# Exp over three PSUM banks instead of two, with single banks for VectorE's scores and for the outputs

## The chip, the cores and the metric

The kernel runs on one core of a Trainium2 chip. Its engines work side by side, each through its own instructions in a fixed order: TensorE (PE in the profile) multiplies matrices and writes to PSUM, ScalarE (ACT) computes functions such as exp, VectorE (DVE) and GpSimd (POOL) compute element by element, and SyncE (SP) here only issues transfers. PSUM, where the products land, has eight banks; one holds 512 fp32 values in each of 128 partitions. Engines wait for each other through semaphores.

The metric is the device time in microseconds (us), the median of several executions. The kernel before takes 386.97 us (386.77 to 387.01 in three runs). The profile is of one more execution, and its span of 384.9 us is what its tables and times refer to.

## What is computed

Attention with grouped heads: batch 8, 8 query heads, 2 key and value heads, 1024 positions, 64 values per head.

```python
scale = 1.0 / np.sqrt(head_dim)                      # head_dim = 64
for g in range(n_kv_heads):                          # 2 groups of 4 query heads
    # q_group: (8, 4, 1024, 64); k_group, v_group: (8, 1, 1024, 64)
    scores = scale * np.matmul(q_group, k_group.transpose(0, 1, 3, 2))
    scores_max = np.max(scores, axis=-1, keepdims=True)
    attn = np.exp(scores - scores_max)
    attn = attn / (np.sum(attn, axis=-1, keepdims=True) + 1e-08)
    output[:, q_start:q_end, :, :] = np.matmul(attn, v_group)
```

The kernel leaves out the subtraction of the maximum, which cancels in the quotient and isn't needed for scores of this size.

## The kernel before

The work is cut into 128 *jobs*: a batch, a query head and one half of its queries (512). A job has eight *cells*, one for each 128 keys. For a cell, TensorE makes 128 x 512 scores (one bank of PSUM), one of two engines takes their exp, and TensorE multiplies the result with the values, in four matmuls of 65 columns (64 values and a column of ones, which gives the sum). When all eight cells of a job are added up, VectorE divides by the sum.

The exp is the larger part of the work, and is shared between two engines:

- *A cells* go to ScalarE, two at a time: a tile of two PSUM banks, one ACTIVATE of 1024 columns.
- *D cells* go to VectorE. A first step (P below) turns the score into the bits of a bf16 number near the exp, by one multiply-add with an integer result. Then a correction, a *chain* of steps on a group of ten cells at a time: z is the low seven bits ("and"), y a linear function of z ("line", on GpSimd), y becomes z times y ("prod"), and y is added to the bits ("add").

The order of all this is made beforehand in Python, by a loop that keeps a time for each engine and always takes what can start first. The constants at the top say how many cells a tile of ScalarE has, and how many banks there are for VectorE's scores and for outputs:

```python
A_CELLS, D_BANKS, O_BANKS = (2, 2), 2, 2      # 2 + 2 + 2 + 2 = 8 banks
GROUP, PARTS = 10, 2
CHAIN = ("and", "line", "prod", "add")
ON_POOL = ("line",)

def part(step, m):          # "prod0": the first half of the group's cells
    n = step[-1]
    return slice(0, m) if not n.isdigit() else slice(m * int(n) // PARTS, m * (int(n) + 1) // PARTS)
# ... make_plan: times used for the order
    QK, PV, P1, NORM = 0.216, 0.1225, 0.603, 0.555
    EXP = (0.05, 0.4268)
    FOUR, TWO, POOL_ONE = (0.20, 0.133), (0.16, 0.27), (0.25, 0.43)
    COST = {"and": FOUR, "line": POOL_ONE, "prod": TWO, "add": TWO}
    LIVE_A, LIVE_D, PENDING, PER_JOB, LEAD, RAMP, AHEAD, FIRST_PV = 28, 5, 16, 2, 6, 6, 0.04, 2.0
# ...
```

What the engines run, in the order that was made:

```python
    def score(cell, kind, n, slot, col):                     # TensorE
        # ... kind "A": column col of a tile of ScalarE, else a bank of VectorE
        nc.tensor.matmul(dst, lhsT=ksets[b % 2][:, h // HPG, side, c * 128 : (c + 1) * 128],
                         rhs=qT[(b, h)], start=True, stop=True)

    def exps(n, cells):                                      # ScalarE
        act = nc.scalar.activation(out=pt[:, 0:m], in_=psum.pop(("A", n))[:, 0:m],
                                   func=AF.Exp, scale=scale)

    def exp_bits(cell, n, g, slot):                          # VectorE, P
        nc.vector.tensor_scalar(out=groups[g][:, slot], in0=psum.pop(cell),
            scalar1=bits_scale, scalar2=bits_bias, op0=ALU.mult, op1=ALU.add)

    def exp_curve(g, m, step):                               # the chain
        eng = nc.gpsimd if step in ON_POOL else nc.vector
        # ... and:  z  = pd & 0x7F              (tensor_scalar)
        # ... line: y  = z * CURVE_A / 128 + CURVE_B   (tensor_scalar)
        # ... prod: y  = z * y                  (tensor_tensor)
        # ... add:  pd = pd + y                 (tensor_tensor)

    def output_mms(s, cell, opens, closes, bk):              # TensorE
        for qs in range(NQS):                                # 4
            nc.tensor.matmul(ops_of[s][:, qs, :], lhsT=p_of[cell][:, qs * 128 : (qs + 1) * 128],
                             rhs=vsets[b % 2][:, h // HPG, c, :], ...)

    def normalise(s):                                        # VectorE, RN
        nc.vector.reciprocal(out=rec, in_=o[:, :, D])
        nc.vector.tensor_tensor(out=stage[(b, h)][:, :, side, :], in0=o[:, :, 0:D],
                                in1=rec.unsqueeze(2).to_broadcast([128, NQS, D]), op=ALU.mult)
```

Queries and keys come from HBM as bf16 copies and are turned by transposing transfers; keys are then placed by `place_k` (on SyncE's queue) in sets that have zeros in the other half of the rows. The results of ScalarE lie in a ring in SBUF (`p_ring`), from which TensorE reads them. The first head is loaded in another way, through transposes on TensorE that use PSUM banks which are free at that time (`first_loads`).

Of the kernel before, what the change touches and what calls it, by code (L numbers as in the profile page):

```python
# [11 lines left out]

CURVE_A, CURVE_B = 0.32988085, -0.33401025

A_CELLS, D_BANKS, O_BANKS = (2, 2), 2, 2
GROUP, PARTS = 10, 2
CHAIN = ("and", "line", "prod", "add")
ON_POOL = ("line",)

def part(step, m):  # L20

# [4 lines left out]
def make_plan(nj, nkc):  # L26
# [6 lines left out]

    QK, PV, P1, NORM = 0.216, 0.1225, 0.603, 0.555
    EXP = (0.05, 0.4268)
    FOUR, TWO, POOL_ONE = (0.20, 0.133), (0.16, 0.27), (0.25, 0.43)
    COST = {"and": FOUR, "line": POOL_ONE, "prod": TWO, "add": TWO}
    FROM_PE, FROM_PV, FROM_ACT, FROM_DVE, FROM_POOL = 0.21, 0.16, 0.165, 0.10, 0.15
    LIVE_A, LIVE_D, PENDING, PER_JOB, LEAD, RAMP, AHEAD, FIRST_PV = 28, 5, 16, 2, 6, 6, 0.04, 2.0
    INF = 1e9  # L40
    FIRST_TURN, FIRST_LOAD, EACH_LOAD = 3.3, 4.5, 4.2
    ops = []
    pe = act = dve = 0.0
# [22 lines left out]
    while normed < nj:  # L66
        best = None
# [2 lines left out]
        lead = min(LEAD, job_a // RAMP)  # L70
        job_d = max(job_d, job_a + lead)
        while job_d < nj and (
            taken[job_d] >= PER_JOB or not todo[job_d]
        ):
            job_d += 1
        if job_a < nj:
# [7 lines left out]
        if job_d < nj and job_d <= job_a + lead + 1 and pending < PENDING:  # L84
            if cur or live["D"] < LIVE_D:
                t = max(pe, min(bank), loaded(job_d))
                if t < INF:
                    best = min(best or (INF,), (t, 2, "qk", 1, t))
# [10 lines left out]
        for q, p, kind in ((normq, 0, "norm"), (p1q, 1, "p1"), (chainq, 2, "chain")):  # L99
            if q:  # L100
                at = q[0][0]
                if kind != "chain" or CHAIN[q[0][3]] not in ON_POOL:
                    at = max(dve, at)
                best = min(best or (INF,), (at, p, kind, 0))
        if cur and job_d >= nj and not p1q:
            best = min(best or (INF,), (dve, 9, "flush", 0))
        t, _, kind, arg = best[:4]
# [32 lines left out]
        elif kind == "open":  # L140
            o = first_free(obank_free)
            obank[arg] = o
            obank_free[o] = INF
            open_jobs.append(arg)
            rem[arg] = list(range(nkc))
            next_job += 1
        elif kind == "pv":
            s, c = arg
            cell = s * nkc + c
            opens = len(rem[s]) == nkc  # L150
            rem[s].remove(c)
            done = not rem[s]
            ops.append((t, "pv", s, cell, opens, done, obank[s]))
            pe = t + PV
            h = home[cell]
            uses[h] -= 1
            if not uses[h]:
                live[h[0]] -= 1
            if done:
                open_jobs.remove(s)  # L160
                normq.append((pe + FROM_PV, s))
        elif kind == "norm":
            s = normq.pop(0)[1]
            ops.append((t, "norm", s))
            dve = t + NORM
            obank_free[obank[s]] = dve + FROM_DVE
            normed += 1
        elif kind == "p1":
            _, cell, k = p1q.pop(0)
            if not cur:  # L170
                d_id += 1
                live["D"] += 1
            ops.append((t, "p1", cell, k, d_id, len(cur)))
            dve = t + P1
            bank[k] = dve + FROM_DVE
            cur.append(cell)
            home[cell] = ("D", d_id)
            if len(cur) == GROUP:
                chainq.append((dve, d_id, cur, 0))
                cur = []  # L180
        elif kind == "flush":
            chainq.append((dve, d_id, cur, 0))
            cur = []
        else:
            _, g, cells, step = chainq.pop(0)
# [4 lines left out]
            dve = end if name not in ON_POOL else dve  # L190
            if step + 1 < len(CHAIN):
                at = end
                if (name in ON_POOL) != (CHAIN[step + 1] in ON_POOL):
                    at += FROM_POOL if name in ON_POOL else FROM_DVE
                chainq.insert(0, (at, g, cells, step + 1))
# [9 lines left out]
def kernel(  # L205
# [27 lines left out]
    PIECE = 512  # L233
    WARM = 30
    CAST_GAP = 3.0
    P_TILES = 28
    POOL_DMA = 1.0
    OBSERVE = 8
    scale = 1.0 / math.sqrt(D)
    bits_scale = 128.0 * scale * math.log2(math.e)  # L240
    bits_bias = 128.0 * 127.0
# [17 lines left out]
    first_pool = ctx.enter_context(tc.tile_pool(name="firstp", bufs=1))  # L259
    qT_pool = ctx.enter_context(tc.tile_pool(name="qTpool", bufs=10))  # L260
    kT_pool = ctx.enter_context(tc.tile_pool(name="kTpool", bufs=4))
    pd_pool = ctx.enter_context(tc.tile_pool(name="pdpool", bufs=5))
    tmp_pool = ctx.enter_context(tc.tile_pool(name="tmppool", bufs=2))
    ostage_pool = ctx.enter_context(tc.tile_pool(name="ostage", bufs=6))
    recip_pool = ctx.enter_context(tc.tile_pool(name="recip", bufs=10))
# [29 lines left out]
    def at(t, f, *args):  # L295
        events.append((t, len(events), f, args))
# [59 lines left out]
    def first_loads():  # L356
# [86 lines left out]
    def score(cell, kind, n, slot, col):  # L443
        b, h, side = jobs[cell // NKC]
        c = cell % NKC
        if kind == "A":
            if col == 0:
                psum[("A", n)] = apools[slot].tile([128, 2, QBS], FP32, name=f"aps{slot}")
# [3 lines left out]
        last_score[0] = nc.tensor.matmul(  # L452
            dst,
            lhsT=ksets[b % 2][:, h // HPG, side, c * 128 : (c + 1) * 128],
            rhs=qT[(b, h)],
            start=True,
            stop=True,
        ).ins

    def exps(n, cells):  # L460
        pt = p_ring[:, n % P_TILES]
        m = len(cells)
        act = nc.scalar.activation(  # L463
            out=pt[:, 0:m], in_=psum.pop(("A", n))[:, 0:m], func=AF.Exp, scale=scale
        )

        exp_ins.append(act.ins)
        if n >= P_TILES and n % OBSERVE == 0:
# [18 lines left out]
    def exp_curve(g, m, step):  # L487
# [7 lines left out]
        if step.startswith("and"):  # L495
            eng.tensor_scalar(  # L496
                out=z, in0=pd, scalar1=0x7F, scalar2=None, op0=ALU.bitwise_and
            )
# [71 lines left out]
    for b in range(B):  # L570
        for h in range(H):
# [8 lines left out]
            if h % HPG == 0:  # L580
# [4 lines left out]
                    at(th - 11.0 - 15.0 * spare + n, transpose_k, b, g, n)  # L585
                for side in range(2):
                    for parity in range(2):
                        at(th - 6.0 - 9.0 * spare, place_k, b, g, side, parity)
# [46 lines left out]
```

## Time and profile before

| what | value |
|---|---|
| device time, median of 3 | 386.97 us |
| span of the profile | 384.9 us |
| A cells, in ACTIVATEs | 812 in 406 |
| D cells, in groups | 212 in 22 |
| normalisations | 128 |
| granted TensorE clock | full speed |

The page of the profile gives, for each engine, its busy time; the share of the span by engine in the chain of work that ended last, which is followed back from the last instruction; and, for each group of instructions, the line, the engine, what it writes and reads, the count, the busy time and mean duration of one, and the idle time of the engine just before them with what ended it. Instructions of one engine can overlap, so the busy time of a group can be less than the count times the mean. The names: `aps` are ScalarE's score tiles, `dps` VectorE's score banks, `ops` the output banks, `pd` the groups of bits, `ost` the normalised output.

### The profile page before, as it was taken

To read this page: it belongs to the slowest core of one execution; us is meant where nothing else is said; L and a number is where in the kernel's file an instruction comes from. 1 tells how busy PE (TensorE), PEld (TensorE's weight loads), DVE (VectorE), ACT (ScalarE), POOL (GpSimd) and SP (SyncE) were. 2 spreads that over 40 slices of the span, in tenths; PEclk is the share of its full clock that TensorE was granted. 3 is DMA by queue.
4 is the path that set the end of the run, shared out by engine and by line. 5 is a ranking of instruction groups with operands and counts; after the bars stand their busy time and mean duration, and the time that the engine had idled before them with its cause. 6 is when DMAs were issued, how large, how long until landed. Compare 5 with 4: busy or idle time off the path is not lost.

```text
span 384.9 us, 12057 instructions
## 1 busy us (share of the span) xinstructions
PE 368.1 (96%) x5172; PEld 234.5 (61%) x5172; DVE 350.1 (91%) x544; ACT 375.1 (97%) x411; POOL 165.3 (43%) x147
## 2 busy tenths in 40 slices
PE   8879999999999999999999999999999999999985
PEld 6425565656666666666666565666566566666654
DVE  4879999999999999999999999999999999999692
ACT  5999999999999999999999999999999999999994
POOL 5394571716246171625535252535445261531410
PEclk9999999999999999999999999999999999999998
DMA  8888979597859769595865949486584756621213
GB/s 137 152 130 141 141 138 173 113 129 148 128 111 134 132 109 141 123 138 85 151 123 126 125 90 169 74 150 113 119 143 109 111 100 113 109 70 29 71 43 83
DMA packets 102422, 45.49 MB, mean 118 GB/s; under 512 B 63776, under 2 KB 100896, under 8 KB 101120
## 3 DMA queue, kind: packets, MB, share of 16 engines
q1 hardware_dynamic: 82096, 31.21, 37.5%
q0 software_dynamic: 19728, 13.25, 29.8%
q8 instruction: 40, 0.66, 0.8%
q10 hardware_dynamic: 544, 0.26, 0.2%
q14 instruction: 14, 0.11, 0.1%
HBM read 25.17 MB, written 27.00 MB: 136 GB/s over the span
## 4 chain that ended last, share of the span: by engine, by line
ACT 94%; PE 2%; DMA 1%; issue 1%; DVE 0%; SPq 0%; POOLq 0%
ACT p_ring L463 94%; PE ops L522 1%; PE aps L452 1%; DMA fk<-in_k_dram 1%; DMA kset<-kset 1%; SPq L389 0%; DVE ost L538 0%; ACT hk L411 0%; DVE kset L382 0%; DVE qT L427 0%; PE aps L373 0%; DVE rec L535 0%; PE ops L419 0%; PE ops L400 0%; POOLq L433 0%
## 5 line engine op out<-in xcount | busy, mean ns | idle before, releaser
L463 ACT ACTIVATE p_ring<-aps 128x1024 bf16<-128x1024 f32 x406 | 372.4, 1100 | 1.2 <-PE aps L452 1.2
L452 PE MATMUL aps<-qT,kset 128*128 128x512 bf16 x812 | 240.6, 378 | 11.4 <-ACT p_ring L463 8.8
L522 PEld LDWEIGHTS <-p_ring 128*128 128x128 bf16 x3248 | 137.5, 97 | 60.4 <-ACT p_ring L463 0.2
L522 PE MATMUL ops<-vset,p_ring 128*128 128x65 bf16 x3248 | 150.8, 194 | 0.1
L477 DVE TENSOR_SCALAR pd<-dps 128x512 uint16<-128x512 f32 x212 | 138.0, 682 | 13.2 <-PE dps L452 12.3
L500 POOL TENSOR_SCALAR y<-z 128x5120 f16<-128x5120 uint16 (+1 forms) x22 | 94.6, 4301 | 82.7 <-DVE rec L535 45.0
L452 PEld LDWEIGHTS <-kset 128*128 128x128 bf16 x1024 | 82.6, 97 | 58.8 <-issue 26.7
L314 POOL DMA_DIRECT2D scr_q<-in_q_dram x63 | 34.7, 551 | 99.0 <-PE aps L452 47.6
L452 PE MATMUL dps<-qT,kset 128*128 128x512 bf16 x212 | 73.4, 378 | 0.0
L511 DVE TENSOR_TENSOR pd<-pd,y 128x5120 uint16<-128x5120 uint16 (+1 forms) x22 | 59.8, 2719 | 0.1
L509 DVE TENSOR_TENSOR y<-z,y 128x5120 f16<-128x5120 uint16 (+1 forms) x22 | 59.8, 2718 | 0.0
L538 DVE TENSOR_TENSOR ost<-ops,rec 128x256 f32<-128x256 f32 x128 | 54.3, 424 | 4.4
L522 PEld LDWEIGHTS <-pd 128*128 128x128 bf16 x848 | 41.3, 98 | 25.6 <-DVE pd L511 3.6
L522 PE MATMUL ops<-vset,pd 128*128 128x65 bf16 x848 | 48.4, 194 | 0.0
L496 DVE TENSOR_SCALAR z<-pd 128x5120 uint16<-128x5120 uint16 (+1 forms) x22 | 31.7, 1443 | 0.6
L535 DVE RECIPROCAL rec<-ops 128x4 f32<-128x4 f32 x128 | 22.5, 176 | 9.8 <-PE ops L522 8.8
L347 POOL DMA_DIRECT2D vset<-in_v_dram x32 | 24.9, 782 | 0.0
L314 POOL DMA_DIRECT2D scr_k<-in_k_dram x15 | 7.8, 521 | 24.1 <-PE aps L452 16.7
L400 PE MATMUL ops<-blank 128*128 128x128 bf16 x40 | 4.4, 286 | 1.1 <-DVE blank L279 1.1
L400 PEld LDWEIGHTS <-blank 128*128 128x128 bf16 x40 | 3.8, 135 | 1.1 <-DVE blank L279 1.1
L354 POOL DMA_DIRECT2D kset<-kset x6 | 3.2, 537 | 0.0
L411 ACT ACT_TABLE_LOAD x1 | 1.3, 1283 | 1.8 <-issue 1.8
(23 smaller groups left out, 8.7 us busy)
## 6 DMA issues: line engine op xcount, KB each, us to landing
out_dram<-ost SPq DMA_DIRECT2D x63, 256.0 KB, 2.9
scr_q<-in_q_dram POOLq DMA_DIRECT2D x63, 128.0 KB, 3.6
kset<-kT SPq DMA_DIRECT2D x60, 64.0 KB, 3.1
vset<-in_v_dram POOLq DMA_DIRECT2D x32, 64.0 KB, 4.0
scr_k<-in_k_dram POOLq DMA_DIRECT2D x15, 128.0 KB, 3.2
qT<-scr_q SPq DMA_TRANSPOSE x63, 4.0
kset<-kset POOLq DMA_DIRECT2D x7, 128.0 KB, 4.0
fq<-in_q_dram ACTq DMA_DIRECT2D x2, 128.0 KB, 3.2
```

Of the source, the lines that this page charges most:

```text
L314: dma = nc.gpsimd.dma_start(out=scr.rearrange("(p f) -> p f", f=1024), in_=src.rearrange("(p s) d -> p (s d)", s=1024 // D),)
L347: nc.gpsimd.dma_start(out=vsets[b % 2][:, g, two * NHC : (two + 1) * NHC, 0:D], in_=v[b, g].rearrange("(c p two) d -> two p c d", p=128, t ...
L452: last_score[0] = nc.tensor.matmul(dst, lhsT=ksets[b % 2][:, h // HPG, side, c * 128 : (c + 1) * 128], rhs=qT[(b, h)], start=True, stop=Tr ...
L463: act = nc.scalar.activation(out=pt[:, 0:m], in_=psum.pop(("A", n))[:, 0:m], func=AF.Exp, scale=scale)
L477: nc.vector.tensor_scalar(out=groups[g][:, slot], in0=psum.pop(cell), scalar1=bits_scale, scalar2=bits_bias, op0=ALU.mult, op1=ALU.add,)
L496: eng.tensor_scalar(out=z, in0=pd, scalar1=0x7F, scalar2=None, op0=ALU.bitwise_and)
L500: eng.tensor_scalar(out=y, in0=z, scalar1=CURVE_A / 128.0, scalar2=CURVE_B, op0=ALU.mult, op1=ALU.add,)
L509: eng.tensor_tensor(out=y, in0=z, in1=y, op=ALU.mult)
L511: eng.tensor_tensor(out=pd, in0=pd, in1=y, op=ALU.add)
L522: nc.tensor.matmul(ops_of[s][:, qs, :], lhsT=p_of[cell][:, qs * 128 : (qs + 1) * 128], rhs=vsets[b % 2][:, h // HPG, c, :], start=opens an ...
L535: nc.vector.reciprocal(out=rec, in_=o[:, :, D])
L538: nc.vector.tensor_tensor(out=stage[(b, h)][:, :, side, :], in0=o[:, :, 0:D], in1=rec.unsqueeze(2).to_broadcast([128, NQS, D]), op=ALU.mult,)
```

## The change

ScalarE's two tiles get three banks each, so that one ACTIVATE takes three cells, 1536 columns. Six of the eight banks are then taken; one is left for VectorE's scores and one for outputs. The chains become short: groups of four cells instead of ten, with "prod" and "add" in two halves, and "line" on VectorE too, so that a P or a normalisation needn't wait for a long step. The times from which the order is made, and the limits for it, are set anew. GpSimd, free of "line", now issues the transfers that place keys. In the first loads other banks are used, and half of one key copy is sent earlier, from ScalarE's queue.

```diff
-A_CELLS, D_BANKS, O_BANKS = (2, 2), 2, 2
-GROUP, PARTS = 10, 2
-CHAIN = ("and", "line", "prod", "add")
-ON_POOL = ("line",)
+A_CELLS, D_BANKS, O_BANKS = (3, 3), 1, 1
+GROUP, PARTS = 4, 2
+CHAIN = ("and", "line", "prod0", "prod1", "add0", "add1")
+ON_POOL = ()
@@ make_plan: the times and limits of the order
-    FOUR, TWO, POOL_ONE = (0.20, 0.133), (0.16, 0.27), (0.25, 0.43)
-    COST = {"and": FOUR, "line": POOL_ONE, "prod": TWO, "add": TWO}
+    FOUR, TWO = (0.09, 0.133), (0.05, 0.27)
+    COST = {"and": FOUR, "line": FOUR, "prod": TWO, "add": TWO}
-    LIVE_A, LIVE_D, PENDING, PER_JOB, LEAD, RAMP, AHEAD, FIRST_PV = 28, 5, 16, 2, 6, 6, 0.04, 2.0
+    LIVE_A, LIVE_D, PENDING, PER_JOB, LEAD, RAMP, AHEAD, FIRST_PV = 18, 6, 8, 2, 2, 6, 0, 2.0
-    FIRST_TURN, FIRST_LOAD, EACH_LOAD = 3.3, 4.5, 4.2
+    AHEAD_D, EXTRA, LAST = 0.05, 0, 6
+    FIRST_TURN, FIRST_LOAD, EACH_LOAD = 2.4, 4.5, 4.2
@@ (cut: how chains are taken up in the order)
@@ buffers
-    P_TILES = 28
+    P_TILES = 18
-    OBSERVE = 8
+    OBSERVE = 16
-    pd_pool = ctx.enter_context(tc.tile_pool(name="pdpool", bufs=5))
+    pd_pool = ctx.enter_context(tc.tile_pool(name="pdpool", bufs=6))
-    apools, dbanks, obanks = psum_pools("aps", 2), psum_pools("dps", 2), psum_pools("ops", 2)
-    p_ring = const_pool.tile([128, P_TILES, 2, QBS], BF16)
+    apools = psum_pools("aps", len(A_CELLS))
+    dbanks, obanks = psum_pools("dps", D_BANKS), psum_pools("ops", O_BANKS)
+    p_ring = const_pool.tile([128, P_TILES, max(A_CELLS), QBS], BF16)
@@ place_k
-        nc.sync.dma_start(
+        nc.gpsimd.dma_start(
@@ first_loads
-        tk = [
-            dbanks[0].tile([128, HALF], BF16, name="dps0"),
-            apools[1].tile([128, HALF], BF16, name="aps1"),
-        ]
+        spare = apools[1].tile([128, A_CELLS[1], 2 * QBS], BF16, name="aps1")
+        tk = [dbanks[0].tile([128, HALF], BF16, name="dps0"), spare[:, 0, :HALF]]
-        warm = obanks[1].tile([128, 128], FP32, name="ops1")
+        warm = apools[0].tile([128, 128], FP32, name="aps0")
-        tq = [
-            dbanks[1].tile([128, HALF], BF16, name="dps1"),
-            obanks[0].tile([128, HALF], BF16, name="ops0"),
-        ]
+        tq = [spare[:, 1, :HALF], obanks[0].tile([128, HALF], BF16, name="ops0")]
         nc.scalar.copy(out=qT[(0, 0)][:, : HALF // 2], in_=tq[0][:, : HALF // 2])
+        nc.scalar.dma_start(
+            out=ksets[0][hi, 0, 1, :HALF], in_=ksets[0][lo, 0, 0, :HALF]
+        )
-        nc.gpsimd.dma_start(out=ksets[0][hi, 0, 1, :], in_=ksets[0][lo, 0, 0, :])
+        nc.gpsimd.dma_start(
+            out=ksets[0][hi, 0, 1, HALF:], in_=ksets[0][lo, 0, 0, HALF:]
+        )
@@ (cut: the shape of ScalarE's tile in score(), the ring's waits, empty halves)
```

In the order that comes out, the changed kernel has 827 A cells (275 ACTIVATEs of three and one of two) and 197 D cells in 50 groups.

More of the change, by code (lines that the diff above doesn't have):

```diff
@@ L35, in make_plan @@
     EXP = (0.05, 0.4268)
-    FOUR, TWO, POOL_ONE = (0.20, 0.133), (0.16, 0.27), (0.25, 0.43)
-    COST = {"and": FOUR, "line": POOL_ONE, "prod": TWO, "add": TWO}
+    FOUR, TWO = (0.09, 0.133), (0.05, 0.27)
+    COST = {"and": FOUR, "line": FOUR, "prod": TWO, "add": TWO}
     FROM_PE, FROM_PV, FROM_ACT, FROM_DVE, FROM_POOL = 0.21, 0.16, 0.165, 0.10, 0.15
-    LIVE_A, LIVE_D, PENDING, PER_JOB, LEAD, RAMP, AHEAD, FIRST_PV = 28, 5, 16, 2, 6, 6, 0.04, 2.0
+    LIVE_A, LIVE_D, PENDING, PER_JOB, LEAD, RAMP, AHEAD, FIRST_PV = 18, 6, 8, 2, 2, 6, 0, 2.0
     INF = 1e9
-    FIRST_TURN, FIRST_LOAD, EACH_LOAD = 3.3, 4.5, 4.2
+    AHEAD_D, EXTRA, LAST = 0.05, 0, 6
+    FIRST_TURN, FIRST_LOAD, EACH_LOAD = 2.4, 4.5, 4.2
     ops = []
-    pe = act = dve = 0.0
+    pe = act = dve = pool = two_end = 0.0
     a_free, bank, obank_free = [0.0] * len(A_CELLS), [0.0] * D_BANKS, [0.0] * O_BANKS
@@ L72, in make_plan @@
         while job_d < nj and (
-            taken[job_d] >= PER_JOB or not todo[job_d]
+            taken[job_d] >= PER_JOB + EXTRA * (job_d >= nj - LAST)
+            or not todo[job_d]
         ):
@@ L87, in make_plan @@
                 if t < INF:
-                    best = min(best or (INF,), (t, 2, "qk", 1, t))
+                    best = min(best or (INF,), (t - AHEAD_D, 2, "qk", 1, t))
         for i, s in enumerate(open_jobs):
@@ L98, in make_plan @@
                 best = min(best or (INF,), (at, 3 + len(open_jobs), "open", next_job))
-        for q, p, kind in ((normq, 0, "norm"), (p1q, 1, "p1"), (chainq, 2, "chain")):
+        for q, p, kind in ((normq, 0, "norm"), (p1q, 1, "p1")):
             if q:
[L101 to L104, printed above, removed]
+                best = min(best or (INF,), (max(dve, q[0][0]), p, kind, 0))
+        for i, (at, _, _, step) in enumerate(chainq):
+            if CHAIN[step] in ON_POOL:
+                at = max(at, pool, two_end)
+            else:
+                at = max(at, dve, pool)
+            best = min(best or (INF,), (at, 2 + i, "chain", i))
         if cur and job_d >= nj and not p1q:
@@ L184, in make_plan @@
         else:
-            _, g, cells, step = chainq.pop(0)
+            _, g, cells, step = chainq.pop(arg)
             ops.append((t, "chain", g, len(cells), CHAIN[step]))
@@ L189, in make_plan @@
             end = t + fixed + each * len(cells[part(name, len(cells))])
-            dve = end if name not in ON_POOL else dve
+            if name in ON_POOL:
+                pool = end
+            else:
+                dve = two_end = end
             if step + 1 < len(CHAIN):
@@ L194, in make_plan @@
                     at += FROM_POOL if name in ON_POOL else FROM_DVE
-                chainq.insert(0, (at, g, cells, step + 1))
+                chainq.insert(arg, (at, g, cells, step + 1))
             else:
@@ L447, in score @@
             if col == 0:
-                psum[("A", n)] = apools[slot].tile([128, 2, QBS], FP32, name=f"aps{slot}")
+                psum[("A", n)] = apools[slot].tile(
+                    [128, A_CELLS[slot], QBS], FP32, name=f"aps{slot}"
+                )
             dst = psum[("A", n)][:, col, :]
@@ L467, in exps @@
         exp_ins.append(act.ins)
-        if n >= P_TILES and n % OBSERVE == 0:
+        if n >= P_TILES and (n - P_TILES) % OBSERVE == 0:
             seen = exp_ins[n - P_TILES + OBSERVE - 1]
@@ L494, in exp_curve @@
         pd, z, y = groups[g][:, cells], temps[g][0][:, cells], temps[g][1][:, cells]
-        if step.startswith("and"):
+        if cells.start == cells.stop:
+            pass
+        elif step.startswith("and"):
             eng.tensor_scalar(
@@ L587 @@
                     for parity in range(2):
-                        at(th - 6.0 - 9.0 * spare, place_k, b, g, side, parity)
+                        at_pool(th - 6.0 - 9.0 * spare, place_k, b, g, side, parity)
                 for two in range(2):
```

## The prediction

> **What bounds the kernel now.** I read the page from its first part (busy shares), then the chain of work that ended last, then the groups of instructions, then the timeline of a steady stretch and of both ends.
>
> ```profile
> PE 368.1 (96%) x5172; PEld 234.5 (61%) x5172; DVE 350.1 (91%) x544; ACT 375.1 (97%) x411; POOL 165.3 (43%) x147
> ```
>
> ```profile
> ACT 94%; PE 2%; DMA 1%; issue 1%; DVE 0%; SPq 0%; POOLq 0%
> ```
>
> ```profile
> L463 ACT ACTIVATE p_ring<-aps 128x1024 bf16<-128x1024 f32 x406 | 372.4, 1100 | 1.2 <-PE aps L452 1.2
> ...
> L477 DVE TENSOR_SCALAR pd<-dps 128x512 uint16<-128x512 f32 x212 | 138.0, 682 | 13.2 <-PE dps L452 12.3
> L500 POOL TENSOR_SCALAR y<-z 128x5120 f16<-128x5120 uint16 (+1 forms) x22 | 94.6, 4301 | 82.7 <-DVE rec L535 45.0
> ```
>
> The exps on ScalarE are 372.4 us of a 384.9 us span, with 1.2 us of idle time before them, and they are 94% of the chain. So the path is: a head until the first exp (6.47 us), the exps back to back, and a tail behind the last one (it ends at 379.3, the span at 384.9: 5.6 us). VectorE is next: 57.0 to 57.6 us of each 60 us in the middle, 95%, and it waits mostly at the two ends. The row of PE is modelled, so I count its issue times below.
>
> Two paces come from the timeline: that of an exp, and that of VectorE's steps one behind another.
>
> ```profile
> 149.06 13.93 ACT L463 ACTIVATE p_ring<-aps 128x1024 bf16<-128x1024 f32 x15
> ```
>
> ```profile
> 201.31 1.28 DVE L477 TENSOR_SCALAR pd<-dps 128x512 uint16<-128x512 f32 x2
> 202.51 0.17 DVE L535 RECIPROCAL rec<-ops 128x4 f32<-128x4 f32 x1
> 202.72 0.42 DVE L538 TENSOR_TENSOR ost<-ops,rec 128x256 f32<-128x256 f32 x1
> 203.06 0.17 DVE L535 RECIPROCAL rec<-ops 128x4 f32<-128x4 f32 x1
> ...
> 203.61 1.28 DVE L477 TENSOR_SCALAR pd<-dps 128x512 uint16<-128x512 f32 x2
> 204.92 1.49 DVE L496 TENSOR_SCALAR z<-pd 128x5120 uint16<-128x5120 uint16 x1
> 206.33 0.17 DVE L535 RECIPROCAL rec<-ops 128x4 f32<-128x4 f32 x1
> ...
> 212.40 2.82 DVE L509 TENSOR_TENSOR y<-z,y 128x5120 f16<-128x5120 uint16 x1
> ```
>
> Fifteen exps take 13.93 us, the last one 1.10 long: (13.93 - 1.10) / 14 = 0.917 us from end to end. On VectorE an instruction starts some 0.08 us before the end of an earlier one that it doesn't depend on: two score steps (P) take 1.20 from start to start of what follows, 0.60 each though one is 0.68 long; a normalisation (RN) takes 0.55; the 5120-wide z step 1.41 (1.49 long). A step that needs the one just before starts behind its end (the P that ended at 204.89, z at 204.92): 0.11 dearer than an overlapped one.
>
> **What the Trainium skill says.** "ScalarE: Activation LUTs", section "What ACT_TABLE_LOAD costs": an ACTIVATE runs at 0.833 ns per element. For 1024 that is 853 ns, so of the 917 measured some 63 ns are fixed. "VectorE: DVE Perf Modes", section "The TRN2 errata": each instruction on this engine pays a fixed cost, so many small tiles pay it many times. The trace agrees: the product of 5120 columns takes 2815 ns, that of 1024 takes 681, five of which would be 3405. "SBUF — State Buffer", section "Who interferes with whom": GpSimd shares a port pair with VectorE's fast modes, and the one that comes second blocks. Here the DMA issues on GpSimd have a median of 520 ns and take up to 1411 ns beside a z step, while the z step keeps 1480 to 1495 ns: GpSimd loses, VectorE doesn't. "Perfetto Trace Analysis", section "Matmuls" of "Optimizing Tensor Performance": independent matmul groups should rotate through different PSUM banks so that the evacuation of one overlaps the next; the change takes this away for VectorE's scores and for the outputs.
>
> **The change, part by part.** The order of instructions in the built kernel gives the counts.
>
> *ScalarE.* 275 exps of three banks and one of two, for 827 blocks (128 keys by 512 queries) instead of 812, since VectorE takes 197 instead of 212. One of three banks: 0.063 + 1536 x 0.000833 = 1.343 us, an estimate from the 0.917 and the skill's rate. 275 x 1.343 + 0.92 = 370.3, against 372.4: only 2.1 us less. 135 or so fixed costs are saved (8.5 us), and 15 more blocks (15 x 0.43 = 6.5) eat most of it.
>
> *VectorE.* Pitches where nothing is waited for: P 0.60; z and y of 2048 columns: 0.69 long (between 420 ns for 1024 and 1494 for 5120), so 0.61; prod and add halves of 1024 columns: 0.68 long, 0.60. Sum: 197 x 0.60 = 118.2; 98 x 0.61 = 59.8; 196 x 0.60 = 117.6; 128 x 0.55 = 70.4; the last small group 1.3. Together 367.3, against 212 x 0.60 + 21 x (1.41 + 2 x 2.73) + 70.4 + 1.7 = 343.6 before: 24 us more, though it has 15 blocks fewer, from the line step that came over from GpSimd and from short instructions. In the new order 57 steps stand directly behind the one they need (37 times z behind its fourth P, 17 times prod behind y): 57 x 0.11 = 6.3. So 373.6 us of work without any wait for TensorE, as long as ScalarE's.
>
> *One bank for VectorE's scores.* From P to the next P: 0.68 for P, 0.04 to TensorE, 0.38 for the score matmul, some 0.09 to VectorE: 1.19 us at best (the 0.04 and 0.09 are gaps at such handovers in this trace). 84 of the 197 P have a single step between them and the P before, which gives 0.60 + 0.55 to 0.61 = 1.15 to 1.21 us. Nothing is spare there, so whatever TensorE is behind in its queue is added to VectorE's time.
>
> *One bank for outputs.* From TensorE's last output matmul of a job to the first of the next: 0.16 until it lands (0.19 long, 0.03 apart), 0.03 to VectorE, 0.21 and 0.42 for RN, 0.04 back: 0.86 us, plus what VectorE still has to finish (a step of up to 0.68). Between the two TensorE has three score matmuls in 45 jobs (3 x 0.215 = 0.65), four in 73 (0.86), more in 6. TensorE's own sum is 1024 x 0.215 + 4096 x 0.031 = 347 us, 93% of ScalarE's 370, so about 24 us can be lost before it matters.
>
> *Head and tail.* The first score goes to the bank that a copy of the first loads reads until 6.02, and the first exp needs three more: 6.02 + 0.05 + 4 x 0.215 + 0.2 = 7.1 instead of 6.47, but the idle time of 0.47 us before the exp at 9.80, where TensorE had waited for the moved keys, should go, as half of them are sent earlier. Behind the last pair of scores stand 26 output blocks and four normalisations that take turns with them: 26 x 0.123 + 4 x 0.85 + 3.5 for the last store = 10.1 us, against 7.4 before (from 377.55); counted from the end of the exps 8.0 instead of 5.6.
>
> *Sum.* ScalarE alone: 7.1 + 370.3 + 8.0 = 385.4 us, against 384.9. The measured time is 2.1 above the profile's span, so 387.5. VectorE alone: first P at about 6.9, 373.6 less the last four normalisations (2.2), and the same tail: 386.3, before any wait. Two engines of equal length coupled by single banks don't both run full. I put 0.06 to 0.1 us on each of the 84 tight P loops (5 to 8 us), half of it hidden, and 1 to 2 us for outputs: about 391 in the span, **393 us measured**.
>
> **The rivals.** *ScalarE stays the bound and nothing is lost* (387 to 389): a round of one tile is 1.53 for the exp from start to end, 0.07 to TensorE, 0.81 for three scores and 0.10 back, 2.5 us, and it has two exps, 2.69, to do it; the half steps are there so that a P or RN never waits long. Against it: VectorE has no slack. *TensorE becomes the bound through the one output bank* (400 to 408): if RN falls anywhere in a VectorE step, 0.3 us on average, 128 x 0.3 + 45 x 0.21 = 48 us are lost, 24 more than it has. For it: the windows of three scores are shorter than 0.86. Against it: it waits for ScalarE's tiles anyway, and these waits can be the same ones. *A real gain* (under 380): needs an exp of three banks below 1.32 us or a much shorter head; I see neither. GpSimd, rid of 94.6 us of line steps but given 60 key copies, stays far from a bound.
>
> **Range and chances.** From ScalarE's 386.5 at the low end to half of the TensorE rival, 404, at the high end. Over 2% faster is below 379.2: 3%. Over 2% slower is above 394.7: 41%. Within: 56%.
>
> **What would show it.** Right: an exp pace of 1.34 us; idle time of ScalarE before its exps that waits for aps, 5 us or more where it was 1.2; VectorE busy near 372 to 378 with P waiting for dps; TensorE waiting for the normalisation. Wrong: ScalarE without gaps and a time under 386, or an exp pace at 1.33 or less; gaps above 15 us with TensorE waiting mostly for ost would mean the second rival.

## The result, and the profile after

The changed kernel takes 407.4 us (407.1 to 409.2), against 387.0 for the kernel before on the same chip: 1.0538 times as long, with a 95% interval of 1.0507 to 1.0568. It is slower by 20 us, and outside the predicted range of 386.5 to 404.

The busy times and the chain of the changed kernel's page:

```profile
PE 379.4 (94%) x5172; PEld 223.8 (55%) x5172; DVE 376.8 (93%) x761; ACT 380.3 (94%) x281; POOL 105.5 (26%) x185
...
DVE 57%; PE 34%; issue 4%; ACT 2%; DMA 1%; ACTq 0%
```

ScalarE, 94% of the chain before, is 2% of it now. The chain runs to and fro between VectorE and TensorE. The groups of instructions (busy time and mean ns of one, then the idle time of the engine before them):

```profile
L475 ACT ACTIVATE p_ring<-aps 128x1536 bf16<-128x1536 f32 (+1 forms) x276 | 377.5, 1461 | 13.6 <-PE aps L464 11.4
...
L489 DVE TENSOR_SCALAR pd<-dps 128x512 uint16<-128x512 f32 x197 | 135.3, 687 | 11.1 <-PE dps L464 9.6
```

ScalarE now stands idle for 13.6 us before its exps, 11.4 of them for scores, where it was 1.2. The table of waits says who holds whom (us in total, times, the longest); the longer rows of GpSimd's transfers, which are issued far ahead, are left out:

```profile
PEld L536 <- DVE ost L552: 68.2, 119, 1.3
...
ACT p_ring L475 <- PE aps L464: 11.4, 36, 1.6
DVE pd L489 <- PE dps L464: 9.6, 37, 0.6
PE ops L536 <- DVE ost L552: 9.6, 26, 1.2
...
PE aps L464 <- ACT p_ring L475: 3.8, 11, 0.5
```

In 119 of the 127 changes of job, the load of the first weights of a new job waits for the normalised output (`ost`) of the job before. By this table TensorE waits for a tile of ScalarE only 3.8 us. The weight loads overlap matmuls, so 68.2 us is not all lost. I added up the gaps of the matmuls themselves in front of each job's first output matmul, beyond their ordinary spacing, over 114 jobs in the middle: 0.222 us each, 28.4 us for 128 (30.3 us when all 127 changes are added up, head and tail included).

One such change in the timeline (start, duration, engine; what ended an idle time in brackets):

```profile
202.47 0.18 DVE L549 RECIPROCAL rec<-ops 128x4 f32<-128x4 f32 x1
...
202.68 0.42 DVE L552 TENSOR_TENSOR ost<-ops,rec 128x256 f32<-128x256 f32 x1
...
203.16 0.30 PE L536 MATMUL ops<-vset,pd 128*128 128x65 bf16 x4 [0.36 <-DVE ost L552]
...
203.29 0.78 PE L536 MATMUL ops<-vset,p_ring 128*128 128x65 bf16 x20
...
203.91 0.38 PE L464 MATMUL aps<-qT,kset 128*128 128x512 bf16 x1
204.12 0.38 PE L464 MATMUL dps<-qT,kset 128*128 128x512 bf16 x1
204.34 0.59 PE L464 MATMUL aps<-qT,kset 128*128 128x512 bf16 x2
...
204.97 5.48 ACT L475 ACTIVATE p_ring<-aps 128x1536 bf16<-128x1536 f32 x4 [0.35 <-PE aps L464]
```

The normalisation ends at 203.10, and TensorE, idle, starts at 203.16 with the six output cells that its order has next. Only then, at 203.91, come the scores that ScalarE needs. They land at 204.93, and ScalarE has been idle for 0.35 us.

ScalarE's own account closes with it. Its exps complete every 1.343 us (the last line: four in 5.48 us, the last of them 1.45 long), so the work is 370.3 us; from the first exp (7.32) to the end of the last (396.85) are 389.5, and 19.2 of these are lost. (The page's 13.6 is less, since the record of an exp overlaps the next by up to 0.2 us, and shorter delays hide in that.) The head is 0.85 us longer than before, the tail 8.65 instead of 5.6.

### The profile page after: what moved, and what is told of

Same layout as the page of the kernel before. It is cut to its first block, busy times and chain, and to the rows that moved or that the text cites. A ratio compares the mean times of both kernels' runs of the same rounds, so it can differ in the third digit from the quotient of the medians.

```text
span 405.5 us, 12103 instructions
## 1 busy us (share of the span) xinstructions
PE 379.4 (94%) x5172; PEld 223.8 (55%) x5172; DVE 376.8 (93%) x761; ACT 380.3 (94%) x281; POOL 105.5 (26%) x185
## 4 chain that ended last, share of the span: by engine, by line
DVE 57%; PE 34%; issue 4%; ACT 2%; DMA 1%; ACTq 0%
PE ops L536 18%; DVE pd L489 18%; DVE ost L552 12%; PE aps L464 11%; DVE y L523 8%; DVE pd L525 7%; DVE rec L549 4%; PE dps L464 4%; DVE z L510 4%; DVE y L514 3%; ACT p_ring L475 2%; PE aps L408 1%; DMA kset<-kset 1%; DMA out_dram<-ost 1%; PE dps L381 0%
## 5 line engine op out<-in xcount | busy, mean ns | idle before, releaser
L475 ACT ACTIVATE p_ring<-aps 128x1536 bf16<-128x1536 f32 (+1 forms) x276 | 377.5, 1461 | 13.6 <-PE aps L464 11.4
L464 PE MATMUL aps<-qT,kset 128*128 128x512 bf16 x827 | 236.0, 378 | 4.4 <-ACT p_ring L475 3.8
L536 PEld LDWEIGHTS <-p_ring 128*128 128x128 bf16 x3308 | 127.5, 97 | 40.4 <-DVE ost L552 12.6
L536 PEld LDWEIGHTS <-pd 128*128 128x128 bf16 x788 | 35.3, 97 | 66.2 <-DVE ost L552 55.6
L523 DVE TENSOR_TENSOR y<-z,y 128x1024 f16<-128x1024 uint16 (+1 forms) x99 | 65.5, 681 | 0.6
L525 DVE TENSOR_TENSOR pd<-pd,y 128x1024 uint16<-128x1024 uint16 (+1 forms) x99 | 64.8, 680 | 0.0
L514 DVE TENSOR_SCALAR y<-z 128x2048 f16<-128x2048 uint16 (+1 forms) x50 | 34.0, 681 | 0.1
L510 DVE TENSOR_SCALAR z<-pd 128x2048 uint16<-128x2048 uint16 (+1 forms) x50 | 33.9, 679 | 0.0
L344 POOL DMA_DIRECT2D kset<-kT x60 | 33.1, 560 | 1.8 <-DMA kset<-kset 0.7
L408 PE MATMUL aps<-blank 128*128 128x128 bf16 x40 | 4.5, 291 | 1.1 <-DVE blank L289 1.1
```

The source lines that it names most:

```text
L344: nc.gpsimd.dma_start(out=ksets[b % 2][side * D : (side + 1) * D, g, side, parity * HALF : (parity + 1) * HALF], in_=kT[(b, g)][parity * D ...
L464: last_score[0] = nc.tensor.matmul(dst, lhsT=ksets[b % 2][:, h // HPG, side, c * 128 : (c + 1) * 128], rhs=qT[(b, h)], start=True, stop=Tr ...
L510: eng.tensor_scalar(out=z, in0=pd, scalar1=0x7F, scalar2=None, op0=ALU.bitwise_and)
L514: eng.tensor_scalar(out=y, in0=z, scalar1=CURVE_A / 128.0, scalar2=CURVE_B, op0=ALU.mult, op1=ALU.add,)
L523: eng.tensor_tensor(out=y, in0=z, in1=y, op=ALU.mult)
L525: eng.tensor_tensor(out=pd, in0=pd, in1=y, op=ALU.add)
```

## The experiments

Theory A: the single output bank makes TensorE wait out each normalisation. Theory B: the single score bank makes VectorE late. Theory C: VectorE simply has too much to do. The first four runs gave banks back, or took work from VectorE, and had the order made anew. The number of VectorE's cells was held at 197 by a limit per job in the first three. Where ScalarE's *loss* is given, it is counted as above: the time from the first exp to the end of the last, less the exps at 1.343 us (three banks) or 0.917 (two) each.

**Two output banks, tiles of three and two**

```diff
-A_CELLS, D_BANKS, O_BANKS = (3, 3), 1, 1
+A_CELLS, D_BANKS, O_BANKS = (3, 2), 1, 2
-            taken[job_d] >= PER_JOB + EXTRA * (job_d >= nj - LAST)
+            taken[job_d] >= (1 if job_d * 6 % 13 < 6 else 2)
```

> The changed kernel with one of ScalarE's tiles cut to two banks and the bank so freed given to the outputs (tiles of 3 and 2 banks, one score bank, two output banks). The number of cells on VectorE is held at 197 and its steps stay the same, so VectorE has the same work. ScalarE needs 165 x 1.343 + 166 x 0.917 = 373.8 us for its exps, 4 more than in the changed kernel. Theory A (the single output bank: TensorE waits out each normalisation): the waits of TensorE for the normalised output, 78 us in the changed kernel, fall below 10, and the time to 390 to 396. Theory B (the single score bank makes VectorE late): still 403 or more, with TensorE's waits moved to VectorE's results. Theory C (VectorE simply has too much to do, 374 us and more, in a fixed order): 400 or more.

Measured: 424.4 us, 1.097 times before (1.0954 to 1.0987). The waits for the normalised output did fall to 9, as A had it, but the time rose far above A's 396. In the new order 85 of ScalarE's tiles have a score for VectorE between their own, and ScalarE waits 20.7 us for scores. The run tells nothing of the bank by itself.

**Two score banks, tiles of three and two**

```diff
-A_CELLS, D_BANKS, O_BANKS = (3, 3), 1, 1
+A_CELLS, D_BANKS, O_BANKS = (3, 2), 2, 1
```

(with the same limit on VectorE's cells)

> The same, but the freed bank is given to VectorE's scores (tiles of 3 and 2 banks, two score banks, one output bank), again with 197 cells on VectorE. Theory A: 403 to 412, the waits for the normalised output stay at 60 us or more. Theory B: 390 to 396, VectorE's waits for scores (9.6 us) vanish and so do most of ScalarE's gaps. Theory C: 400 or more, with waits for the normalised output that are shorter than in the changed kernel.

Measured: 441.2 us, 1.1403 (1.1386 to 1.142). The waits for the normalised output stay (75 us), but the time is far above the ranges of A and B, and C had named no upper end; again a new order, with 73 tiles interrupted by a score for VectorE.

**The old banks**

```diff
-A_CELLS, D_BANKS, O_BANKS = (3, 3), 1, 1
+A_CELLS, D_BANKS, O_BANKS = (2, 2), 2, 2
```

(with the same limit)

> The banks of the kernel before (tiles of two banks, two score banks, two output banks) with everything else as in the changed kernel: chains of four in half steps, all on VectorE, 197 cells. ScalarE alone needs 413 x 0.917 + 0.5 = 379.2 us, with head and tail 393, 395 measured. Theory A: 394 to 398, ScalarE without gaps. Theory B: the same. Theory C: 402 or more, as VectorE's load is that of the changed kernel.

Measured: 408.0 us, 1.0544 (1.0529 to 1.056), as C would have it. But the timeline shows something else:

```profile
200.72 0.38 PE L464 MATMUL aps<-qT,kset 128*128 128x512 bf16 x1
...
200.93 0.59 PE L464 MATMUL dps<-qT,kset 128*128 128x512 bf16 x2
...
201.36 0.38 PE L464 MATMUL aps<-qT,kset 128*128 128x512 bf16 x1
...
201.78 9.27 ACT L475 ACTIVATE p_ring<-aps 128x1024 bf16<-128x1024 f32 x10 [0.20 <-PE aps L464]
```

Two scores for VectorE stand between the two of one tile of ScalarE, which starts 0.20 us late. I come back to this below.

**The line step back on GpSimd, banks as changed**

```diff
-ON_POOL = ()
+ON_POOL = ("line",)
-    FOUR, TWO = (0.09, 0.133), (0.05, 0.27)
-    COST = {"and": FOUR, "line": FOUR, "prod": TWO, "add": TWO}
+    FOUR, TWO, POOL_ONE = (0.09, 0.133), (0.05, 0.27), (0.25, 0.43)
+    COST = {"and": FOUR, "line": POOL_ONE, "prod": TWO, "add": TWO}
```

> The changed kernel with its banks (3, 3, 1, 1), but the line step of each chain back on GpSimd: about 30 us less work on VectorE (50 x 0.61), with 200 cells instead of 197. Theory A: the loop through the single output bank stays, and is only a little shorter since VectorE is free more often when a job ends: 400 to 407. Theory B: 402 to 407. Theory C: 388 to 393.

Measured: 413.1 us (410.6 to 415.9), 1.07 (1.0633 to 1.0767). The two longer of the four executions ran at a granted clock of 0.977, the two shorter at 1.0. VectorE is busy 352.0 us instead of 376.8, and the kernel is not faster: against C. The time is above all three forecasts, though. The waits for the normalised output stay at 77 us:

```profile
PEld L536 <- DVE ost L552: 62.8, 104, 1.2
...
PE ops L536 <- DVE ost L552: 13.9, 31, 1.0
```

ScalarE loses 16.1 us where it lost 19.2 in the changed kernel. What makes the run longer is its tail, 16.2 us behind the last exp instead of 8.65; this wasn't followed up.

The lesson of these four was that the order must not change. So the next runs free banks without touching it: ScalarE's second tile keeps its three score matmuls and its exp of 1536 columns, but has one physical bank, which is written three times and read three times. Values change, the sequence and the sizes don't.

```diff
-                psum[("A", n)] = apools[slot].tile(
-                    [128, A_CELLS[slot], QBS], FP32, name=f"aps{slot}"
+                psum[("A", n)] = apools[slot].tile(
+                    [128, (3, 1)[slot], QBS], FP32, name=f"aps{slot}"
-            dst = psum[("A", n)][:, col, :]
+            dst = psum[("A", n)][:, 0 if slot else col, :]
@@ exps: the input of the second tile
+        src = src[:, 0:m] if src.shape[1] > 1 else src.to_broadcast([128, m, QBS])
@@ (cut: pools of two banks, other banks in first_loads)
```

**Same order, a second output bank**

```diff
-            ops_of[s] = obanks[bk].tile([128, NQS, E1], FP32, name=f"ops{bk}")
+            ops_of[s] = obanks[s % 2].tile([128, NQS, E1], FP32, name=f"ops{s % 2}")
```

> The changed kernel with every engine's instructions in the same order and of the same sizes, but jobs take turns in two output banks. The bank comes from ScalarE's second tile, which has only one physical bank here: its three score matmuls write that bank one after another, and the exp reads it three times, so those values are not attention's and the timing of each instruction stays. Theory A (TensorE waits out each normalisation in the single output bank): the waits for the normalised output, 78 us, nearly vanish, ScalarE's lost 19 us go, and the time falls from 407 to 388 to 394. Theory B (single score bank) and theory C (VectorE's work, 374 us at best in this order): 402 to 407; under C the waits only move from TensorE's outputs to VectorE's results.

Measured: 387.5 us, 1.0005 (0.9999 to 1.0012): the 20 us are gone. From this run's page:

```profile
PE 370.7 (96%) x5172; PEld 236.5 (61%) x5172; DVE 370.2 (96%) x761; ACT 374.3 (97%) x281; POOL 105.8 (27%) x185
...
L477 ACT ACTIVATE p_ring<-aps 128x1536 bf16<-128x1536 f32 (+1 forms) x276 | 371.6, 1509 | 2.2 <-PE aps L464 1.8
```

ScalarE's waits are 2.2 us, and of the waits for `ost` a single one of 0.2 us is left. ScalarE's loss is 2.0 us. VectorE does all its work with one score bank and is at 96%.

**Same order, a second score bank**

```diff
-            dst = psum[cell] = dbanks[n].tile([128, QBS], FP32, name=f"dps{n}")
+            n = turn[0] = 1 - turn[0]
+            dst = psum[cell] = dbanks[n].tile([128, QBS], FP32, name=f"dps{n}")
```

> The same with one output bank, but VectorE's scores take turns in two banks; ScalarE's second tile again in one physical bank. Theory A: 403 to 408, the waits for the normalised output stay. Theory B: 388 to 394, and VectorE's 9.6 us of waits for scores vanish. Theory C: 402 or more.

Measured: 408.1 us, 1.0539 (1.0517 to 1.0561): nothing gained. Its waits:

```profile
PEld L538 <- DVE ost L554: 69.4, 120, 1.3
...
DVE pd L491 <- PE dps L466: 9.6, 37, 0.7
```

Even VectorE's own waits for scores stay at 9.6 us. They didn't come from the score bank; TensorE, held up by the output bank, is late with the scores (with the second output bank they were 2.7 us). B falls. This run also has ScalarE's second tile in one physical bank, so that stand-in isn't what made the run before fast.

**Same order, both second banks**

(both edits)

> The same with two output banks and two score banks. Theory A: as with the second output bank alone, within 3 us. Theory B: as with the second score bank alone. If both single banks share the loss: 387 to 390 here and about 397 for each alone. Theory C: 400 or more even here, since VectorE has the same steps in the same order.

Measured: 386.5 us, 0.9979 (0.9972 to 0.9986), 1 us less than with the output bank alone, as A had it. This is about what the three-bank tiles can reach with 197 cells on VectorE.

**The bank held for a shorter time: the reciprocal left out**

```diff
-        nc.vector.reciprocal(out=rec, in_=o[:, :, D])
-        nc.vector.tensor_tensor(out=stage[(b, h)][:, :, side, :], in0=o[:, :, 0:D],
-            in1=rec.unsqueeze(2).to_broadcast([128, NQS, D]), op=ALU.mult)
+        nc.vector.tensor_scalar(out=stage[(b, h)][:, :, side, :], in0=o[:, :, 0:D],
+            scalar1=1.0 / S, scalar2=None, op0=ALU.mult)
```

> The changed kernel with its banks and its order, but the reciprocal left out of each normalisation and the output multiplied by a constant (it is not divided by the sum). The output bank is held 0.21 us less for each of 128 jobs, and VectorE has 128 x 0.21 = 27 us less to do. Theory A: 407 minus 20 to 27 us, 380 to 388. Theory B: 402 to 407. Theory C: 385 to 392; a later run with as much work taken from VectorE elsewhere tells A from C.

Measured: 388.0 us, 1.0017 (1.001 to 1.0023), with all single banks. The read of the bank takes 0.42 us instead of 0.64. TensorE's gaps in front of a job's first output matmul shrink from 28.4 to 3.3 us. This takes work from VectorE too, so the next run takes a little more, elsewhere.

**As much work taken from VectorE elsewhere: the line step left out**

```diff
-        if cells.start == cells.stop:
+        if cells.start == cells.stop or step == "line":
-            eng.tensor_tensor(out=y, in0=z, in1=y, op=ALU.mult)
+            eng.tensor_tensor(out=y, in0=z, in1=z, op=ALU.subtract)
```

> The changed kernel with its banks and its order, but the line step left out of every chain on VectorE (the product is replaced by a difference that is zero, at the same size, so the correction is left out of the values): 50 x 0.61 = 30 us less for VectorE, slightly more than leaving out the reciprocal took, while the output bank is held for the same steps. Theory A: only a shorter wait in front of the normalisation can help, 396 to 405. Theory C: as without the reciprocal, 385 to 391.

Measured: 403.9 us, 1.0432 (1.0417 to 1.0448), 3.6 us less than the changed kernel. Its page and its waits, beside the page of the run without the reciprocal (first):

```profile
PE 371.3 (96%) x5172; PEld 236.0 (61%) x5172; DVE 354.8 (92%) x633; ACT 373.9 (97%) x281; POOL 105.4 (27%) x185
```

```profile
PE 379.6 (94%) x5172; PEld 224.3 (56%) x5172; DVE 347.6 (86%) x711; ACT 379.8 (95%) x281; POOL 101.6 (25%) x185
...
PEld L536 <- DVE ost L552: 64.1, 118, 1.0
```

Here VectorE has less to do than there (347.6 against 354.8) and the kernel is 16 us slower. C falls; what counts is for how long the bank is held.

**The order made with the true hold**

```diff
-            obank_free[obank[s]] = dve + FROM_DVE
+            obank_free[obank[s]] = dve + FROM_DVE + 0.085
```

> The changed kernel with one number of the order's making corrected: the output bank counts as free 0.085 us later, as the trace of the changed kernel has it from the start of a job's last output matmul to the first of the next (0.93 us against 0.845 in the order's own times, without any wait). 198 cells on VectorE. Theory A, with the order's understatement as the main part of the loss: 390 to 398. Theory A, with the length of the hold itself as the main part (there is not enough other work for TensorE in it, whatever the order): 401 to 410. Theory C: 403 or more.

Measured: 404.9 us, 1.046 (1.0444 to 1.0475). The new order takes 2.5 us less: ScalarE's loss falls from 19.2 to 14.3 us, but the tail grows from 8.65 to 11.6. So with an order that knows the true hold most of the loss stays, and the length of the hold is the main part.

**Two tries at a shorter hold in a whole kernel**

VectorE only copies the outputs out of PSUM; GpSimd makes the inverse (as a power of -1) and the product. First in the changed kernel's order, then with the order made anew for it (`NORM = 0.345`).

```diff
+        nc.vector.tensor_copy(out=raw, in_=o)
-        nc.vector.reciprocal(out=rec, in_=o[:, :, D])
+        nc.gpsimd.tensor_tensor(out=rec, in0=raw[:, :, D], in1=minus, op=ALU.pow)
-        nc.vector.tensor_tensor(
+        nc.gpsimd.tensor_tensor(
@@ (cut: the tiles raw and minus, and raw as the product's input)
```

> A whole kernel again: the changed kernel with its order, where VectorE only copies the 260 outputs of a job out of PSUM (0.42 us long) and GpSimd makes the inverse and the product in SBUF. The output bank is held some 0.2 us less and VectorE has 27 us less to do. Theory A: 386 to 391, as without the reciprocal. If GpSimd's reads of SBUF hold up VectorE's two-input steps: 395 or more, with longer prod and add steps.

> The same, with the order made anew for a VectorE step of 0.345 instead of 0.555 at the end of a job: 210 cells go to VectorE and 271 exps of three banks and one of one stay, 364.5 us for ScalarE, 6 less than in the changed kernel. Theory A: 379 to 386 if ScalarE is the bound. If VectorE's load decides in a fixed order (210 x 1.5 + 128 x 0.345 = 360 us at least): 388 or more.

Measured: 402.8 us, 1.0399 (1.0379 to 1.042), and 409.1 us, 1.057 (1.0554 to 1.0585), both far above what A gave. In the first:

```profile
L553 POOL TENSOR_TENSOR rec<-raw,minus 128x4 f32<-128x4 f32 x128 | 160.9, 1257 | 4.1 <-DVE raw L551 2.4
...
L525 DVE TENSOR_TENSOR y<-z,y 128x1024 f16<-128x1024 uint16 x98 | 69.1, 724 | 0.6
L527 DVE TENSOR_TENSOR pd<-pd,y 128x1024 uint16<-128x1024 uint16 x98 | 68.7, 726 | 0.0
L551 DVE COPY raw<-ops 128x260 f32<-128x260 f32 x128 | 53.9, 421 | 7.5 <-PE ops L538 6.0
```

GpSimd takes 1257 ns for four inverses and is busy 368 us in all, and VectorE's two-input steps rise from 684 to 724 ns. The read of the bank is as short as without the reciprocal (0.42), but the copy starts 0.35 us after the last output has landed instead of 0.21, and TensorE loses about 15 us instead of 3.3. The second expectation, longer steps and a time above 395, is what came. But the longer steps are not shown to be the whole cause. From the eleventh job on, the copy also waits for GpSimd, which read the buffer that it now writes again, and it then starts 0.105 us after the landing at the earliest, against 0.037 in the first ten jobs. And 5.3 of the 14.7 us between the two runs are in the tail (12.6 us behind the last exp against 7.3), where GpSimd's inverse and product follow the last copy. Made anew, the order gives 210 cells to VectorE, which is then busy 384.6 us, and it loses more.

**The interrupted tiles**

What was left open is why the old banks with the new chains also took 408. In three runs the turns are set as in the kernel before, so that no tile of ScalarE is interrupted by a score for VectorE. First the old banks with everything else changed (banks and limit as in the run of the old banks above):

```diff
-    LIVE_A, LIVE_D, PENDING, PER_JOB, LEAD, RAMP, AHEAD, FIRST_PV = 18, 6, 8, 2, 2, 6, 0, 2.0
-    AHEAD_D, EXTRA, LAST = 0.05, 0, 6
+    LIVE_A, LIVE_D, PENDING, PER_JOB, LEAD, RAMP, AHEAD, FIRST_PV = 18, 6, 8, 2, 2, 6, 0.04, 2.0
+    AHEAD_D, EXTRA, LAST = 0, 0, 6
```

> The banks of the kernel before with the changed chains took 408.0 us, 13 above what its exps need (395). In its order 64 of ScalarE's 414 tiles have one or two scores for VectorE between their two scores, since the changed settings give VectorE's scores the first turn; the kernel before has none. Here the settings for the turns are those of the kernel before (0.04 for ScalarE's, 0 for VectorE's), everything else as in that run; no tile is interrupted any more, 196 cells on VectorE, 414 exps of two banks. If the interrupted tiles caused the loss: 394 to 398. If the chains on VectorE did (steps of four cells, 374 us of work): 402 or more.

Measured: 394.5 us, 1.0198 (1.0183 to 1.0213), which fits the interrupted tiles as the cause. The order is a new one here too, but the trace of the old banks says the same: of the 15.2 us that ScalarE lost there, 13.4 are lost in front of its 64 interrupted tiles. Now it loses 1.5 us and the exps are back to back:

```profile
L475 ACT ACTIVATE p_ring<-aps 128x1024 bf16<-128x1024 f32 x414 | 380.4, 1111 | 2.0 <-PE aps L464 1.5
```

Then the kernel before with nothing but the new chains (with their times, ten buffers for groups instead of five, and the limit on VectorE's cells):

```diff
-GROUP, PARTS = 10, 2
-CHAIN = ("and", "line", "prod", "add")
-ON_POOL = ("line",)
+GROUP, PARTS = 4, 2
+CHAIN = ("and", "line", "prod0", "prod1", "add0", "add1")
+ON_POOL = ()
```

> The kernel before with one thing changed: chains of four cells in half steps, all on VectorE, with their times in the order, ten buffers for groups, and 196 cells on VectorE; its banks, limits, lead, ring and first loads stay. ScalarE needs 414 x 0.917 = 379.6 us and with head and tail 392, 394 measured. If VectorE's 374 us of short steps fit beside that: 393 to 397. If they don't: 402 or more.

Measured: 394.5 us, 1.0195 (1.0178 to 1.0212): what 414 exps of two banks take. The chains cost little or nothing beyond the cells that VectorE no longer takes. At last the changed kernel itself with uninterrupted tiles (the edit of the first of the three):

> The changed kernel with the settings for the turns of the kernel before, so that none of ScalarE's tiles is interrupted (79 times in the changed kernel); 195 cells on VectorE. The windows between two jobs' output matmuls keep three scores in 47 jobs and four in 69. If the output bank's hold causes the loss whatever the turns: 402 to 410. If the interrupted tiles do: 388 to 396.

Measured: 406.1 us, 1.0501 (1.0486 to 1.0517), with 84 us of waits for the normalised output:

```profile
PEld L536 <- DVE ost L552: 72.8, 118, 1.2
...
PE ops L536 <- DVE ost L552: 11.5, 42, 0.7
```

With tiles of two banks and two output banks the turns are worth 13 us, with one output bank 1. In the changed kernel 17 of ScalarE's 19 lost us stand in front of its 79 interrupted tiles. But with a second output bank the same 79 tiles cost next to nothing (a loss of 2.0 us in all), and without any interrupted tile the single output bank still costs ScalarE 17.6. So in the changed kernel the interruption mostly decides where TensorE's delay shows, and is not what makes it.

## Why the prediction was wrong

ScalarE's sum held and VectorE's was 4 us too long; what failed is the way in which the engines' waits add up.

- *ScalarE*: an exp of three banks was put at 1.343 us and completes every 1.343. Head 7.32 against 7.1, tail 8.65 against 8.0.
- *ScalarE alone would give 387.5*: with a second output bank, in the same order, it is 387.5. That it agrees to the digit is luck: there the tail is 6.3 us instead of 8.0, and 2.0 us are lost in between.
- *VectorE*: busy 376.8, inside the 372 to 378 named, but only with its waits: with both second banks it does the same steps in 369.5. The 373.6 had counted 57 steps as standing "directly behind the one they need". Of the 37 times that z is behind a P, 36 have a P of the next group there, and in the trace such a z starts 0.083 us before the P ends, like any other. 36 x 0.11 = 4.0 us of the 6.3 were never due. And "Two engines of equal length coupled by single banks don't both run full" is wrong as far as the score bank goes. With one score bank and two for outputs both run at 96 and 97%. The 84 tight loops, for which 5 to 8 us were put down, cost at most the 1 us between the runs with one and with two score banks.
- *The step that failed* is "1 to 2 us for outputs". It cost 20: TensorE stood 28.4 us and ScalarE lost 19.2. The view that this was small rested on two terms: "about 24 us can be lost before it matters", and "it waits for ScalarE's tiles anyway, and these waits can be the same ones". TensorE does have that slack: with the second output bank its gaps in front of scores, counted as the 28.4 were but over the whole run, are 28.8 us. In the changed kernel they are still 17.8. So only 11 us of the stalls took the place of waits it has anyway, and the rest passed on to ScalarE. The order is fixed, and in nearly all jobs what follows a late normalisation is four to six output cells and only then ScalarE's next scores.
- *The rival named for this had the right mechanism and the right time* (400 to 408), and I gave it too little weight. Its parts were near: a hold of 0.86 us without a wait, measured 0.93 (0.19 to land, 0.04, 0.64 for the normalisation, 0.06 back); a wait of 0.3 for VectorE's step in progress, measured 0.21 (0.25 from landing to the read, of which 0.04 is the handover). Its 48 us of stalls are 28 to 30 in the trace, and of its 24 us of slack 11 were used. That the time came out right is in part luck, as both terms were too large: 48 - 24 = 24 us, where 20 were lost.
- *The gain of the change itself* was small from the start, as the sum said: the fixed cost saved by longer exps goes back into 15 more cells, and both second banks together, which this PSUM can't hold, would give 0.2%.

The split of the 20 us is shown by single edits in one order (a second bank 19.9, the reciprocal's 0.21 us 19.4, 29 us of VectorE's work 3.6). Why the orders made anew for tiles of three and two are so slow was not followed up; about half of ScalarE's loss there (20 of 37 us with two output banks, 28 of 53 with two score banks) is in front of interrupted tiles. No kernel measured here that computes the whole attention is faster than the one before.

## What to carry to other kernels

A bank that is accumulated into and then read by another engine is a round trip: add up landing, handover, the wait for the step in progress, the read and the way back, and compare that with the work which the fixed order puts between. If it is longer, the writing engine stands still at each change, and only part of that is made up by waits it has anyway (here 11 of 30 us). Less load on the reading engine hardly helped here (29 us less brought 3.6); a second bank or a shorter read brought 19 to 20. When only one of several parts is to be judged and a scheduler makes the order, free the resource inside the old order, since the remade order can cost more than the part under test (424 and 441 us here, from a kernel of 407).

## What the runs showed of the hardware that was not expected

- VectorE can be kept at 96% in 761 short instructions with a single score bank, with TensorE at 96 and ScalarE at 97% beside it, and each step at the length it has elsewhere (P 685 ns, the two-input halves 684 and 683, as in the changed kernel).
- A power of -1 over 4 columns on GpSimd takes 1257 ns on average, a product over 256 columns 759, beside a VectorE that is busy 92%.
- In the run in which GpSimd is busy 92% instead of 26%, with operands in SBUF, two-input steps of 1024 columns on VectorE take 724 ns on average instead of 684, and the steps z and y of 2048 columns 746 and 731 instead of 687 and 689. A P, which reads PSUM, stays at 685 to 687.
